# Summing four column groups of a modulation vector with adding transfers in DRAM instead of TensorE transposes

## The chip, the cores and the metric

The kernel runs on one core of a Trainium2 chip. The core has five engines with queues of their own: TensorE (PE in the profile; PEld is its loading of the stationary operand), VectorE (DVE), ScalarE (ACT), GpSimd (POOL) and SyncE (SP, which here only issues transfers). Each engine takes its instructions in order; semaphores hold one back until what it needs is there. The metric is the device time of one execution in microseconds (us).

## The reference

One layer of a hybrid backbone in fp32 over 512 latent tokens of width 1024, with 256 context tokens. What matters here is the modulation: one vector-matrix product gives six vectors of 1024 values, of which the last four (`gt1`, `sh2`, `sc2`, `gt2`) are used late in the layer.

```python
mod = jax.nn.silu(c) @ w_mod[l] + b_mod[l]
sh1, sc1, gt1, sh2, sc2, gt2 = jnp.split(mod[:, None, :], N_MOD, axis=-1)
h_lat = modulate(x, norm1_g[l], sh1, sc1)
...
# the token mixer: Mamba-2 scan and window attention, each projected, gated, then one output projection
out_lat = (g_ssd * (y_ssd @ w_o_ssd) + g_att * (y_att @ w_o_att)) @ w_out
x = x + gt1 * o_lat
x = x + gt2 * conv_ffn(modulate(x, norm2_g[l], sh2, sc2), w_up[l], ...)
return rmsnorm(x, final_g)
```

## The kernel before, in words

**Products.** Every fp32 product is made of three matmuls: each operand is split into a high part (rounded to the PE's fast format) and the rest. `gemm` issues wh x xh (L237), wh x xl (L238) and wl x xh (L240), eight groups of three for a block of 128 rows by 512 tokens: 24 matmuls of 512 columns. Below, such a block is a half of an `os` step (the projection of the scan's output, two halves for each of eight row blocks) or a whole `out` step (the output projection).

**Weights.** They come in pieces of 512 KB. `load_raw` issues one on SP (L177) into a raw buffer, the tile `wraw`, of which there are three; ACT casts it to the high part (`whi`, L183), and DVE subtracts to get the rest (`wlo`, L184). The function of both is `split`. A raw buffer is free, and SP issues the next load, when its last reader has ended.

**The second modulation.** The four late vectors are 4096 values, in eight column groups (cg 0 to 7) of 512. `m_step(i)` is step i of 32; group cg has the steps 4 cg to 4 cg + 3. A step's load (`wm`, 512 KB through the same three raw buffers) carries two blocks of 128 input rows by 512 columns. DVE multiplies each block by a scalar for each partition and adds it to the accumulator `acc`, the tile `tm` (L794 for a group's first block, L796 for the seven others). `tm` has one buffer (L113). After a group's last step `acc` still has to be summed over its 128 partitions: PE transposes it in four pieces into a PSUM bank (L800), DVE sums along the free axis (L802) and adds the bias (L803) into four columns of `mod2`. Groups 0 and 1 give the first gate, 2 and 3 the second norm's shift, 4 and 5 its scale, 6 and 7 the second gate.

**The order of the work.** A list at the end of the program gives the stages: the `os` steps 3 to 7 with the m-steps 10 to 17 woven in (10 with the first, 11 and 12, 13, 14 and 15, 16 and 17), the `out` steps 0 to 4 with the m-steps 18 to 23, `vectors` (which makes the scale vector `a2` of groups 4 and 5), the last `out` steps, the second norm, the `up` steps with the m-steps 24 to 31 beside the first eighteen of them, and the `down` steps. A scheduler then sets each engine's order from dependencies and its own idea of when things are ready; on the chip that order is fixed.

**The merge.** After an `os` step, DVE multiplies by a gate (L1787) and adds the attention branch (L1788), ACT casts the result to `mh` (L1789) and DVE makes the rest `ml` (L1790). Step o gives tile o of `mh` and `ml`; an `out` step reads all eight, tile 7 last. The gates themselves are made by L1780 and L1781 on DVE from rows loaded by SP (L1775).

**The gate as a row.** `row_tiles` takes groups 6 and 7 and needs them along the free axis: PE transposes (L2060), DVE copies (L2061), SP writes 4 KB to DRAM (L2062) and loads rows from there, spread over all partitions (L2067, L2068). It stands beside the third `up` step from the end.

GpSimd's queue has no work between the scan's last use near 743 us and the second norm's near 854 us, and none from there to the down stage.

Of the kernel before, what the change touches and what calls it, by code (L numbers as in the profile page):

```python
# [9 lines left out]
F32 = mybir.dt.float32  # L10
# [3 lines left out]
ALU = mybir.AluOpType  # L14
# [4 lines left out]
P = 128  # L19
# [8 lines left out]
V_BMOD = 0  # L28
# [11 lines left out]
def raw(ap):  # L40
    return ap.bitcast(F32)
# [3 lines left out]
def tile_hybrid_layer(  # L45
# [32 lines left out]
    V, S, G, T = nc.vector, nc.scalar, nc.gpsimd, nc.tensor  # L78
# [5 lines left out]
    dpool = ctx.enter_context(tc.tile_pool(name="dpool", bufs=1, space=DRAM))  # L84
# [25 lines left out]
    def misb():  # L110
        return bank("mis")
# [3 lines left out]
    def tmp(tag):  # L115
        return tpool.tile([P, 512], F32, tag=tag, name=tag, bufs=TMP[tag])
# [27 lines left out]
    for j, t in enumerate((wdn[0], DSUMS[1], DSUMS[2], DSUMS[5], DSUMS[4], wdn[1], wdn[3])):  # L144
        for u in range(DU):
            n = min(2, DK - 2 * u) * HC
# [11 lines left out]
    QUEUED = mybir.DependencyInfo(mybir.DependencyClass.NoSync, mybir.DependencyReason.SCHED_ONLY)  # L158
# [22 lines left out]

    def split(r, n, hi, lo):
        F["cast"] = S.copy(hi[:, :n], r[:, :n])  # L183
        return V.tensor_tensor(lo[:, :n], r[:, :n], raw(hi[:, :n]), ALU.subtract)  # L184

    ELSEWHERE = {}
    SCALED = {("dn", 40), ("dn", 41)}
# [1 line left out]
    def load(key):  # L189
        r, n = load_raw(key)  # L190
        if key[0] == "m":
            return r
        if key in SCALED:
            for z in range(0, n, 512):
                V.tensor_tensor(r[:, z : z + 512], r[:, z : z + 512], rows_["g"][1], ALU.mult)
        if key in ELSEWHERE:
            hi, lo = ELSEWHERE[key]()
            split(r, n, hi, lo)
            return hi, lo
        if key[0] == "dn" and key[1] % 4 > 1:  # L200
            if "dnw" not in F:
                F["dnw"] = hpool.tile([P, 2, 2, 1024], F32R, tag="hll", name="dnw")
            hi, lo = (F["dnw"][:, key[1] % 2, i, :] for i in range(2))
        else:
            hi = wpool.tile([P, 1024], F32R, tag="whi", name="whi", bufs=2)
            lo = wpool.tile([P, 1024], F32R, tag="wlo", name="wlo", bufs=2)
        split(r, n, hi, lo)
        return hi, lo
# [13 lines left out]
    def weave(a, b):  # L222
        r, n, m = [], len(a), len(b)
        for i in range(n):
            r.append(a[i])
            r += b[i * m // n : (i + 1) * m // n]
        return r
# [18 lines left out]
    vec = cpool.tile([P, NV], F32, name="vec")  # L246
# [13 lines left out]
    mod2 = cpool.tile([P, 32], F32, name="mod2")  # L260
# [165 lines left out]
    with tc.tile_pool(name="spool", bufs=1) as sp:  # L426
# [235 lines left out]
        r = {}  # L662
        cq = tmp("te")[:, :LC]
        for j in range(KT):
# [46 lines left out]
            x = ("hi", "lo") if j >= NU else ("hh", "hl")  # L711
# [31 lines left out]
        for n in range(2):  # L743
            for j in range(KT):
                x = ("hi", "lo") if j >= NU else ("hh", "hl")
# [33 lines left out]
        return [("g", i)], fn  # L779

    macc = {}

    def m_step(i):
        cg, kk = i // 4, i % 4

        def fn(r):
            if kk == 0:
                macc[0] = tmp("tm")
            acc = macc[0]
            for u in range(2):  # L790
                k = 2 * kk + u
                sc = csil[:, k, 0:1]
                if k == 0:
                    V.tensor_scalar_mul(acc, r[:, 0:512], sc)  # L794
                else:
                    V.scalar_tensor_tensor(acc, r[:, u * 512 : u * 512 + 512], sc, acc, ALU.mult, ALU.add)  # L796
            if kk == 3:
                ps = misb()
                for c in range(4):
                    T.transpose(ps[:, c * P : (c + 1) * P], acc[:, c * P : (c + 1) * P], ident)  # L800
                z = slice(4 * cg, 4 * cg + 4)
                V.tensor_reduce(mod2[:, z], ps.rearrange("p (c q) -> p c q", c=4), axis=AX.X, op=ALU.add)  # L802
                V.tensor_tensor(mod2[:, z], mod2[:, z], vec[:, V_BMOD + 16 + 4 * cg : V_BMOD + 20 + 4 * cg], ALU.add)  # L803

        return [("m", i)], fn
# [71 lines left out]
    Q, F = {}, {}  # L877
# [957 lines left out]
    a2 = cpool.tile([P, 8], F32, name="a2")  # L1835

    def vectors():
        V.scalar_tensor_tensor(a2, mod2[:, 16:24], 1.0, vec[:, V_N2 : V_N2 + 8], ALU.add, ALU.mult)

    HL = L // 2  # L1840
# [154 lines left out]
    def up_step(t):  # L1995
        def fn(wa, wb):
            pa, pb = accb(), accb()
            if t == 0:

                with tc.manual_schedule(engines={mybir.EngineType.PE}):  # L2000
                    def product(ps, w, k, u):
                        c, z, st, en = slice(k * P, (k + 1) * P), HALF[u], u == 0 and k == 0, k == KT - 1
                        for v, y in ((0, h2h), (1, h2h), (0, h2l)):
                            T.matmul(
                                ps[:, z], w[v][:, c], y[:, k, z],
                                start=st and v == 0 and y is h2h, stop=en and y is h2l, skip_group_check=True,
                            )

                    for k in range(KT):
                        norm2_k(k, 0)  # L2010
                        if k == 2:
                            F["rs2"] = half_root(F["pf"], F["sq2"], 1)
                        if k == 5:
                            F["r2"].append(rms_spread(F["rs2"], 2))
                        product(pa, wa, k, 0)
                        product(pb, wb, k, 0)
                    for k in range(KT):
                        norm2_k(k, 1)
                        product(pa, wa, k, 1)
                        product(pb, wb, k, 1)  # L2020
                a = up_first(pa, pb, t)
            else:
                gemm([(pa, h2h, h2l)], wa)
                a = up_first(pa, pb, t)
                gemm([(pb, h2h, h2l)], wb)
            up_second(a, pb, t)

        return [("up", t), ("up", NFF + t)], fn

    def x1_turn(c):  # L2030

        def fn():
            t = tmp("te")
            V.transpose(t, x1[c // 4][:, c % 4, :])
            for a in range(4):
                o = x1_d[:, c * P + 32 * a : c * P + 32 * a + 32].rearrange("(f i) j -> i f j", i=32)
                nc.sync.dma_start(o, t[32 * a : 32 * a + 32, :].rearrange("i (f j) -> i f j", j=32))

        return [], fn
# [10 lines left out]
    x1_rows = [], x1_load  # L2050
# [3 lines left out]
    rows_ = {}  # L2054

    def row_tiles():
        V.tensor_copy(g2c[:, 0:4], mod2[:, 24:28])
        V.tensor_scalar_mul(g2c[:, 4:8], mod2[:, 28:32], -1.0)
        ps, t = misb(), tmp("te")
        T.transpose(ps[0:8, 0:P], g2c, ident)  # L2060
        V.tensor_copy(t[0:8, 0:P], ps[0:8, 0:P])  # L2061
        nc.sync.dma_start(g2_d.rearrange("(c p) -> c p", p=P), t[0:8, 0:P])  # L2062
        tiles = [hpool.tile([P, HC], F32, tag=t, name="row" + t) for t in ("q2", "ssq", "rbc4")] + [tmp("tm")]
        rows_["g"], rows_["f"] = tiles[:2], tiles[2:]
        for i in range(2):
            z = slice(HC * i, HC * i + HC)
            nc.sync.dma_start(rows_["f"][i], fg_d[z].partition_broadcast(P))  # L2067
            nc.sync.dma_start(rows_["g"][i], g2_d[z].partition_broadcast(P))  # L2068
# [150 lines left out]
    def down_step(j, u):  # L2219
        tail = j == 6 and u == 2  # L2220

        def fn(*w):
# [37 lines left out]
        + weave([os_step(o) for o in range(3, 8)], msteps[10:18])  # L2260
        + weave([out_step(o) for o in range(5)], msteps[18:24])
        + [([], vectors)]
        + [([("out", o) for o in (5, 6, 7)], out_last), ([], close_c1)]
        + weave(
            weave([up_step(t) for t in range(18)], msteps[24:]) + [up_step(t) for t in range(18, NFF)],
            [([], lambda: None)] * 6 + [x1_turn(c) for c in range(8)] + [x1_rows] + [([], lambda: None)] * 4 + [([], row_tiles)] + [([], lambda: None)] * 2,
        )
        + [down_step(j, u) for j in range(7) for u in range(3 if j == 6 else DU)],
        early=("g", 15),
# [86 lines left out]
```

## Time and profile before

| | |
|---|---|
| time, median of 3 runs | 1219.94 us (1219.82 to 1220.01) |
| the profiled execution: time, span | 1219.4 us, 1217.6 us |
| PE busy | 1208.7 us, granted clock 0.998 |
| DVE, ACT, POOL busy | 924.4, 679.6, 204.8 us |
| moved by transfers | 214.71 MB |

The span runs from the first instruction to the last. A line of a group gives the code line, engine, operation, the tile written and the tiles read, and how many; in a timeline the two numbers ahead are start and duration in us, and what stands in brackets is the idle time just before and what ended it. `SPq` and `POOLq` are transfers by the engine that issues them; their time to landing runs from issue to the last byte. Matmul durations overlap, since PE is pipelined: the distance of their starts counts.

### The profile page before, as it was taken

The numbers are of one execution on the slowest core, as the hardware profiler recorded it, in microseconds if no ns is written. First come the engines' busy times: TensorE is split into PE (matmuls) and PEld (weight loads), VectorE is DVE, ScalarE is ACT, GpSimd is POOL, SyncE is SP. The second block draws the span as 40 slices with busy tenths as digits, with TensorE's granted clock in tenths as the row PEclk, the third lists the DMA queues.
The fourth block names the chain that finished last, engine by engine and source line by source line (L and its number), as shares of the span: only waits on it lengthen the run. The fifth ranks groups of instructions, "written<-read, shape, count | busy, mean of one in ns | idle before, by whom it ended". The sixth has DMA issues, their size and how long they took to land.

```text
span 1217.6 us, 17462 instructions
## 1 busy us (share of the span) xinstructions
PE 1208.7 (99%) x6296; PEld 993.7 (82%) x6296; DVE 924.4 (76%) x1499; ACT 679.6 (56%) x1263; POOL 204.8 (17%) x223
## 2 busy tenths in 40 slices
PE   9999999999999999999999999999999999999997
PEld 6798888888878868778777778888988888888886
DVE  5857888888566688797896867677787777768777
ACT  5557787778544367486575664223534334346653
POOL 0000121100003544252451631000200000000021
PEclk9999999999999999999999999999999999999999
DMA  9645889844758535346376558777265534337652
GB/s 371 259 137 184 160 242 261 170 148 129 175 160 247 169 87 181 108 133 194 104 167 202 172 188 277 233 238 242 55 159 135 190 109 135 119 115 234 193 187 88
DMA packets 122920, 214.71 MB, mean 176 GB/s; under 512 B 26312, under 2 KB 68368, under 8 KB 122832
## 3 DMA queue, kind: packets, MB, share of 16 engines
q1 hardware_dynamic: 110256, 187.09, 49.0%
q0 software_dynamic: 12288, 26.22, 9.5%
q8 instruction: 50, 0.82, 0.3%
q14 instruction: 38, 0.31, 0.1%
q10 hardware_dynamic: 288, 0.27, 0.1%
HBM read 187.26 MB, written 43.85 MB: 190 GB/s over the span
## 4 chain that ended last, share of the span: by engine, by line
PE 96%; DVE 1%; issue 1%; ACT 1%; DMA 1%; POOL 0%; SPq 0%; POOLq 0%; DVEq 0%; ACTq 0%
PE acc L237 20%; PE acc L240 20%; PE acc L238 20%; PE score L958 3%; PE po L1007 3%; PE pt L994 2%; PE mis L580 2%; PE mis L1687 2%; PE mis L1559 2%; PE mis L1695 1%; PE mis L2217 1%; PE mis L2216 1%; PE mis L2215 1%; PE acc L2217 1%; PE acc L2216 1%; PE acc L2215 1%
## 5 line engine op out<-in xcount | busy, mean ns | idle before, releaser
L183 ACT CAST whi<-wraw 128x1024 fp32r<-128x1024 f32 (+1 forms) x115 | 120.3, 1047 | 160.0 <-PE acc L238 107.0
L184 DVE TENSOR_TENSOR wlo<-wraw,whi 128x1024 fp32r<-128x1024 f32 (+1 forms) x115 | 143.6, 1249 | 68.1 <-ACT whi L183 65.6
L237 PE MATMUL acc<-hlh,whi 128*128 128x512 f32 x472 | 194.0, 411 | 0.0
L238 PE MATMUL acc<-hll,whi 128*128 128x512 f32 x472 | 185.0, 392 | 0.0
L240 PE MATMUL acc<-hlh,wlo 128*128 128x512 f32 x472 | 184.9, 392 | 0.0
L237 PE MATMUL acc<-mh,whi 128*128 128x512 f32 x368 | 143.6, 390 | 0.0
L238 PE MATMUL acc<-ml,whi 128*128 128x512 f32 x368 | 143.2, 389 | 0.0
L240 PE MATMUL acc<-mh,wlo 128*128 128x512 f32 x368 | 143.2, 389 | 0.0
L240 PEld LDWEIGHTS acc<-hlh,wlo 128*128 128x128 f32 x472 | 88.6, 188 | 19.6
L237 PEld LDWEIGHTS acc<-hlh,whi 128*128 128x128 f32 x472 | 88.8, 188 | 18.0 <-issue 2.8
L238 PEld LDWEIGHTS acc<-hll,whi 128*128 128x128 f32 x472 | 88.9, 188 | 17.3 <-issue 2.4
L240 PEld LDWEIGHTS acc<-mh,wlo 128*128 128x128 f32 x368 | 69.1, 188 | 14.5
L237 PEld LDWEIGHTS acc<-mh,whi 128*128 128x128 f32 x368 | 69.1, 188 | 14.4
L238 PEld LDWEIGHTS acc<-ml,whi 128*128 128x128 f32 x368 | 69.1, 188 | 14.2
L967 DVE CUSTOM_DVE_ANT_0 p<-score,winm,nsink 128x512 f32<-128x512 f32 (+1 forms) x64 | 51.8, 810 | 15.4 <-PE score L958 13.9
L1392 DVE SCALAR_TENSOR_TENSOR ta<-acc,half,ta 128x511 f32<-128x511 f32 (+1 forms) x66 | 43.8, 664 | 22.6 <-ACT ta L1391 22.4
L1391 ACT ACTIVATE ta<-acc,half 128x512 f32<-128x512 f32 (+1 forms) x66 | 46.7, 708 | 25.2 <-PE acc L240 23.9
L974 ACT ACTIVATE p<-p,mneg 128x512 f32<-128x512 f32 (+1 forms) x64 | 49.7, 777 | 15.4 <-DVE mneg L967 14.8
L164 POOL DMA_DIRECT2D dsum<-wdn x24 | 25.4, 1143 | 193.0 <-DVE wlo L1091 171.7
L1002 DVE TENSOR_TENSOR ptl<-pt,pth 128x512 fp32r<-128x512 f32 x72 | 47.5, 685 | 8.5 <-ACT pth L998 7.7
L796 DVE SCALAR_TENSOR_TENSOR tm<-wraw,csil,tm 128x512 f32<-128x512 f32 x56 | 43.6, 778 | 13.0 <-DMA wraw<-wm 12.3
L237 PE MATMUL acc<-hch,whi 128*128 128x256 f32 x176 | 53.2, 302 | 0.0
(444 smaller groups left out, 2994.0 us busy)
## 6 DMA issues: line engine op xcount, KB each, us to landing
wraw<-wup SPq DMA_DIRECT2D x44, 512.0 KB, 3.6
dsum<-wdn POOLq DMA_DIRECT2D x24, 704.0 KB, 8.9
wraw<-wm SPq DMA_DIRECT2D x32, 512.0 KB, 4.0
fb<-cs_d SPq DMA_DIRECT2D x32, 512.0 KB, 6.6
wraw<-wx SPq DMA_DIRECT2D x24, 512.0 KB, 3.7
wm<-wm SPq DMA_DIRECT2D x16, 512.0 KB, 8.2
wraw<-wz SPq DMA_DIRECT2D x16, 512.0 KB, 4.2
wraw<-wos SPq DMA_DIRECT2D x16, 512.0 KB, 4.7
```

The costliest lines, as they stand in the source:

```text
L183: F["cast"] = S.copy(hi[:, :n], r[:, :n])
L184: return V.tensor_tensor(lo[:, :n], r[:, :n], raw(hi[:, :n]), ALU.subtract)
L237: T.matmul(ps, wh, xh[:, k0 + k, :], start=a, stop=False)
L238: T.matmul(ps, wh, xl[:, k0 + k, :], start=False, stop=False)
L240: T.matmul(ps, wl, xh[:, k0 + k, :], start=False, stop=b)
L796: V.scalar_tensor_tensor(acc, r[:, u * 512 : u * 512 + 512], sc, acc, ALU.mult, ALU.add)
L958: T.matmul(ps[:, o : o + len(z) * P], Q[h][:, b * P : (b + 1) * P], k[:, j, z[0] * P : (z[-1] + 1) * P], start=v == 0 and o % 512 in (0, P ...
L967: V.tensor_tensor_reduce(p[:, :w], d["ps"][i][:, o0 : o0 + w], m, op0=ALU.add, op1=ALU.min, scale=1.0, scalar=nsink[:, h : h + 1], accum_o ...
L974: S.activation(p, p, AF.Exp, bias=d["mneg"][:, i : i + 1], scale=-1.0, accum_out=d["den"][:, i : i + 1])
L1002: V.tensor_tensor(d["ptl"][x], d["pt"][x], raw(d["pth"][x]), ALU.subtract)
L1391: S.activation(o[:, :n], ps[:, :n], AF.Identity, scale=hcol(base_w, stride + i), bias=hcol(base_b, i))
L1392: x = V.scalar_tensor_tensor(o[:, 1:n], ps[:, 0 : n - 1], hcol(base_w, i), o[:, 1:n], ALU.mult, ALU.add)
```

## The change

Groups 2, 3, 6 and 7 are no longer summed by PE. When such a group's accumulator is complete, `fold` issues nine transfers on GpSimd's queue: one copies `acc` (128 rows of 512 values, 256 KB) to a DRAM tile, seven add the lower half of the rows onto the upper half (64, 32, 16, 8, 4, 2 and 1 rows, `max_dma_last_dim=512` setting the size of their pieces), and one brings the remaining row into four columns of `mod2`. Each waits for the landing of the one before. The bias addition is a function of its own, `folded`, placed later in the program: group 2's in step 20, group 6's in step 31, group 3's in `vectors`, group 7's in `row_tiles`; in the scheduler's order it stands behind the latest split. `row_tiles` itself stands two places later, beside the last `up` step.

```diff
     def split(r, n, hi, lo):
         F["cast"] = S.copy(hi[:, :n], r[:, :n])
-        return V.tensor_tensor(lo[:, :n], r[:, :n], raw(hi[:, :n]), ALU.subtract)
+        F["sub"] = V.tensor_tensor(lo[:, :n], r[:, :n], raw(hi[:, :n]), ALU.subtract)
+        return F["sub"]
...
+    FOLDS = {cg: dpool.tile([P, 512], F32, name="fold%d" % cg) for cg in (2, 3, 6, 7)}
+
+    def fold(cg, acc):
+
+        d, n = FOLDS[cg], P // 2
+        G.dma_start(d, acc)
+        while n:
+            G.dma_start(d[0:n, :], d[n : 2 * n, :], accum_op=ALU.add, max_dma_last_dim=512)
+            n //= 2
+        G.dma_start(mod2[:, 4 * cg : 4 * cg + 4], d[0, :].rearrange("(c p) -> p c", p=P))
+
+    def folded(cg):
+        z = slice(4 * cg, 4 * cg + 4)
+        x = V.tensor_tensor(mod2[:, z], mod2[:, z], vec[:, V_BMOD + 16 + 4 * cg : V_BMOD + 20 + 4 * cg], ALU.add)
+        tc.add_manual_dep(x.ins, F["sub"].ins.name, QUEUED, reason="behind a split")
...
-            if kk == 3:
+            if i in (20, 31):
+                folded({20: 2, 31: 6}[i])
+            if kk == 3 and cg in FOLDS:
+                fold(cg, acc)
+            elif kk == 3:
                 ps = misb()
...
     def vectors():
+        folded(3)
...
     def row_tiles():
+        folded(7)
...
-            [([], lambda: None)] * 6 + [x1_turn(c) for c in range(8)] + [x1_rows] + [([], lambda: None)] * 4 + [([], row_tiles)] + [([], lambda: None)] * 2,
+            [([], lambda: None)] * 6 + [x1_turn(c) for c in range(8)] + [x1_rows] + [([], lambda: None)] * 6 + [([], row_tiles)],
```

The new code moves the lines behind it by some twenty: L794 and L796 become L810 and L812, L1780, L1781, L1787, L1788 and L1790 become L1800, L1801, L1807, L1808 and L1810; L184 stays. On GpSimd's queue the first fold (of group 2) now stands where nothing stood, between the first and the second norm's work; its rows, with the tile `fold` in DRAM and `mod` for `mod2`:

```order
L788 DMA fold_764<-tm 128x512
L790 DMA fold_764<-fold_764 256x128
L790 DMA fold_764<-fold_764 128x128
L790 DMA fold_764<-fold_764 64x128
L790 DMA fold_764<-fold_764 32x128
L790 DMA fold_764<-fold_764 16x128
L790 DMA fold_764<-fold_764 16x64
L790 DMA fold_764<-fold_764 16x32
L792 DMA mod_94<-fold_764 128x4x1
```

Group 3's nine follow directly.

The change also moves DVE's rows. The first place is the middle of `os` steps 6 and 7. Before, from a split of step 6's second weight on, with the four multiplies of the m-steps 14 and 15 (L796, reading `tm` and `wraw`) between splits (L184) and merge operations:

```order
L184 TENSOR_TENSOR wlo<-wraw,whi 128x1024
L796 SCALAR_TENSOR_TENSOR tm<-wraw,csil,tm 128x512
L1787 TENSOR_TENSOR tb<-acc,ld_7598 128x512
L184 TENSOR_TENSOR wlo<-wraw,whi 128x1024
L1788 TENSOR_TENSOR tb<-tb,ld_7600 128x512
L796 SCALAR_TENSOR_TENSOR tm<-wraw,csil,tm 128x512
L1790 TENSOR_TENSOR ml<-tb,mh 128x512
L796 SCALAR_TENSOR_TENSOR tm<-wraw,csil,tm 128x512
L1781 SCALAR_TENSOR_TENSOR ld_7598<-ld_7598,r_s 128x512
L796 SCALAR_TENSOR_TENSOR tm<-wraw,csil,tm 128x512
L184 TENSOR_TENSOR wlo<-wraw,whi 128x1024
```

Now, with the first row step 14's first multiply and the second row the same split as the first row above:

```order
L812 SCALAR_TENSOR_TENSOR tm<-wraw,csil,tm 128x512
L184 TENSOR_TENSOR wlo<-wraw,whi 128x1024
L812 SCALAR_TENSOR_TENSOR tm<-wraw,csil,tm 128x512
L1807 TENSOR_TENSOR tb<-acc,ld_7602 128x512
L812 SCALAR_TENSOR_TENSOR tm<-wraw,csil,tm 128x512
L1808 TENSOR_TENSOR tb<-tb,ld_7604 128x512
L184 TENSOR_TENSOR wlo<-wraw,whi 128x1024
L1810 TENSOR_TENSOR ml<-tb,mh 128x512
L812 SCALAR_TENSOR_TENSOR tm<-wraw,csil,tm 128x512
L1801 SCALAR_TENSOR_TENSOR ld_7602<-ld_7602,r_s 128x512
L1800 SCALAR_TENSOR_TENSOR ld_7604<-ld_7603,ld_7604 128x512
L184 TENSOR_TENSOR wlo<-wraw,whi 128x1024
```

Step 14 has moved from behind that split to ahead of it, and step 15's first multiply from behind the next split to ahead of it.

The second place is the passage from the last `os` step to `out` step 0, on DVE again. Before, from the split of `out` step 0's weight (first row) to the end of the last merge (L1787, L1788, L1790), with the m-steps 18 (second row) and 19 (last row):

```order
L184 TENSOR_TENSOR wlo<-wraw,whi 128x1024
L796 SCALAR_TENSOR_TENSOR tm<-wraw,csil,tm 128x512 x2
L1787 TENSOR_TENSOR tb<-acc,ld_7598 128x512
L1788 TENSOR_TENSOR tb<-tb,ld_7600 128x512
L184 TENSOR_TENSOR wlo<-wraw,whi 128x1024
L1790 TENSOR_TENSOR ml<-tb,mh 128x512
L796 SCALAR_TENSOR_TENSOR tm<-wraw,csil,tm 128x512 x2
```

Now:

```order
L812 SCALAR_TENSOR_TENSOR tm<-wraw,csil,tm 128x512
L184 TENSOR_TENSOR wlo<-wraw,whi 128x1024
L812 SCALAR_TENSOR_TENSOR tm<-wraw,csil,tm 128x512
L1807 TENSOR_TENSOR tb<-acc,ld_7602 128x512
L812 SCALAR_TENSOR_TENSOR tm<-wraw,csil,tm 128x512
L1808 TENSOR_TENSOR tb<-tb,ld_7604 128x512
L184 TENSOR_TENSOR wlo<-wraw,whi 128x1024
L1810 TENSOR_TENSOR ml<-tb,mh 128x512
L812 SCALAR_TENSOR_TENSOR tm<-wraw,csil,tm 128x512
```

Step 18's first multiply has moved ahead of that split, and step 19's between the two halves of the last merge.

## The prediction

> **What bounds the kernel now.** I read the page's head and its chain first: who is busy, and what the end hangs on.
>
> ```profile
> span 1217.6 us, 17462 instructions
> PE 1208.7 (99%) x6296; PEld 993.7 (82%) x6296; DVE 924.4 (76%) x1499; ACT 679.6 (56%) x1263; POOL 204.8 (17%) x223
> PE 96%; DVE 1%; issue 1%; ACT 1%; DMA 1%; POOL 0%; SPq 0%; POOLq 0%; DVEq 0%; ACTq 0%
> ```
>
> TensorE (PE) carries 96% of the chain and never rests. So only two things move the time: PE instructions that go away, and new moments in which PE waits. Then I read the stages in which the change works, by windows, and the transfers of 755 to 845 us, where the second modulation's loads run between the projections' weights.
>
> ```profile
> core 0: us, PE busy (x) PEld busy (x) DVE busy (x) ACT busy (x) POOL busy (x), PEclk, DMA share, GB/s
> 757.00:779.00 22.00, 22.00 (x99) 18.22 (x98) 14.95 (x21) 5.46 (x6) 0.00 (x0) 1.00 0.70 226
> 779.00:801.00 22.00, 22.00 (x101) 18.19 (x100) 14.60 (x22) 5.44 (x6) 0.00 (x0) 1.00 0.75 236
> 801.00:823.00 22.00, 22.00 (x101) 18.19 (x100) 16.99 (x23) 5.99 (x7) 0.00 (x0) 1.00 0.80 251
> ...
> 1060.00:1105.00 45.00, 45.00 (x202) 37.15 (x201) 32.67 (x49) 18.07 (x25) 0.00 (x0) 1.00 0.38 118
> ```
>
> PE is busy for all of each window, POOL (GpSimd) is idle, DVE has a quarter of its time free, and the transfers are dense (0.70 to 0.80) in the first three, thin (0.38) in the up stage.
>
> ```profile
> wraw<-wm SPq DMA_DIRECT2D x13, 512.0 KB, 4.5
> wraw<-wos SPq DMA_DIRECT2D x8, 512.0 KB, 5.0
> ...
> DMA to landing us min/median/max: 3.5/4.7/5.6
> ...
> DVE tm L796 <- DMA wraw<-wm: 2.5, 1, 2.5
> ```
>
> A load of 512 KB takes 4.5 to 5 us here, 3.5 at the best and 5.6 at the worst. Once, DVE stood 2.5 us before an m-step's load, in order, with a weight's split queued behind it. That wait cost PE nothing then; how near it was to costing is the question.
>
> **What is taken away.** One group of transposes, by the timeline of PE:
>
> ```profile
> 779.59 0.39 PE L240 MATMUL acc<-yh,wlo 128*128 128x512 f32 x1
> 779.82 0.60 PE L800 MATMUL mis<-ident,tm 128*128 128x128 f32 x4
> 780.17 0.48 PE L237 MATMUL acc<-yh,whi 128*128 128x512 f32 x1
> 780.49 0.40 PE L238 MATMUL acc<-yl,whi 128*128 128x512 f32 x1
> 780.72 0.40 PE L240 MATMUL acc<-yh,wlo 128*128 128x512 f32 x1
> ...
> 791.64 0.39 PE L240 MATMUL acc<-yh,wlo 128*128 128x512 f32 x1
> ```
>
> Matmuls otherwise start 0.227 apart (779.59, 779.82), so L240 would have come at 780.28 instead of 780.72: 0.44 us a group. Four groups go (column groups 2, 3, 6, 7): 4 x 0.44 = 1.8 us, all of it on PE's path. Four of DVE's sums behind them go too, and their bias additions stay:
>
> ```profile
> 780.62 0.68 DVE L802 TENSOR_REDUCE mod<-mis 128x4 f32<-128x512 f32 x1
> ...
> 781.82 0.15 DVE L803 TENSOR_TENSOR mod<-mod,vec 128x4 f32<-128x4 f32 x1
> ```
>
> 4 x 0.68 us on DVE are worth nothing by themselves, since DVE isn't the bound. The gain of 1.8 us is 0.15%, less than the 0.2% (2.4 us) that a measurement of this kernel can tell from no change.
>
> **What is moved: DVE's order.** This decides. The accumulator tile `tm` has one buffer. Before, PE had to transpose it before the next column group could start; now it is free when the copy to DRAM has landed, and the scheduler places the m-steps of group 3 one projection half earlier: in the rows of the order, step 14's first multiply stood behind the split of the half that PE needs at 791.64, and now stands ahead of it; step 15's stands ahead of the next split, step 18's ahead of out_step 0's, step 19's ahead of the last merge's second half. Each of these waits for a load, and DVE goes in order. And each load is issued only when a raw buffer is free: step 14's when the split before has ended, step 15's when the split behind step 14 has. So load, multiply, split and load form a loop that has to fit in one half of a projection (24 matmuls x 0.2275 = 5.46 us).
>
> ```profile
> 769.59 0.75 DVE L796 SCALAR_TENSOR_TENSOR tm<-wraw,csil,tm 128x512 f32<-128x512 f32 x1
> ...
> 770.97 0.69 DVE L1788 TENSOR_TENSOR tb<-tb,ld 128x512 f32<-128x512 f32 x1
> 771.58 1.22 DVE L184 TENSOR_TENSOR wlo<-wraw,whi 128x1024 fp32r<-128x1024 f32 x1
> ...
> 775.96 0.69 DVE L1781 SCALAR_TENSOR_TENSOR ld<-ld,r_s 128x512 f32<-128x512 f32 x1 [2.56 <-DMA ld<-ts_d]
> ```
>
> With these durations (successive operations overlap by about 0.08), and L for a load:
> - Step 14: L + 0.75 + 1.22 - 0.08 = L + 1.9. Step 15, with L1788 between: L + 2.5. They fit for L under 3.6 and under 3.0.
> - The start: step 12's second multiply comes behind L1781, at 776.57, and ends at 777.3; step 13's load goes out then. Step 13's two multiplies, L1787, L1788 and the split follow its landing: 777.3 + L + 3.75.
>
> I take L = 4.4, just below the median of the m loads: while DVE waits, it frees no buffer, and fewer loads share the engines. Then:
> 1. The split behind step 13 ends at 785.5. PE needs it at 785.76 (5.44 before 791.20, which is 791.64 less the 0.44 of the group that is gone). No stall.
> 2. Step 14: 785.5 + 6.3 = 791.85 against 791.20: 0.65.
> 3. Step 15: 791.85 + 6.9 = 798.75 against 791.85 + 5.46 = 797.3: 1.45.
> 4. Steps 16 and 17: two halves with one late load between, 0 to 1; I take 0.3.
> 5. Step 18 ahead of out_step 0's split: L + 1.9 = 6.3 against 5.46: 0 to 0.85; 0.6.
> 6. Step 19 ahead of the merge. Its rows before:
>
> ```profile
> 813.89 0.39 PE L240 MATMUL acc<-mh,wlo 128*128 128x512 f32 x1
> ...
> 818.20 0.39 PE L237 MATMUL acc<-mh,whi 128*128 128x512 f32 x1
> ...
> 815.45 0.69 DVE L1788 TENSOR_TENSOR tb<-tb,ld 128x512 f32<-128x512 f32 x1
> ...
> 817.20 0.68 DVE L1790 TENSOR_TENSOR ml<-tb,mh 128x512 fp32r<-128x512 f32 x1
> ...
> 816.18 0.62 ACT L1789 CAST mh<-tb 128x512 fp32r<-128x512 f32 x1 [0.98 <-DVE tb L1788]
> ```
>
> PE takes the last of mh's eight tiles 4.31 after out_step 0's split is first used (818.20 - 813.89). Step 19's load is issued when that split ends; mh then needs L + 0.75 + 0.69 + 0.62 = 6.45: late by 2.1; ml comes 0.8 after that beyond PE's next step. Together 2.9 if the split was just in time, less if it had slack; I take 2.5.
>
> Sum: 0.65 + 1.45 + 0.3 + 0.6 + 2.5 = 5.5 of stalls, less 1.8: +3.7 us. The profiled execution took 1219.4 (span 1217.6 and 1.8 around it), 0.5 below the median 1219.94; on the median that gives 1223.6.
>
> Bounds. At L = 3.5 the splits of steps 14 and 15 come at 790.0 and 796.0, in time, and only the merge's wait may be left: 0 to 1. At L = 5.6 the five terms are about 1 + 2 (step 14), 2.6, 1.5, 2 and 4: 13. Against the median: 1218.2 to 1231.
>
> **What is added.** Each fold is nine transfers in a row on GpSimd's queue. No row shows an adding transfer of this size; the nearest are POOL's own:
>
> ```profile
> dsum<-wdn POOLq DMA_DIRECT2D x24, 704.0 KB, 8.9
> ...
> DMA to landing us min/median/max: 3.1/3.2/4.6
> ...
> DMA to landing us min/median/max: 1.8/3.5/7.8
> ...
> L794 DVE TENSOR_SCALAR tm<-wraw,csil x3: 478/479/483, 781.9 to 827.7; 128x512 f32<-128x512 f32 x3
> ...
> L184 DVE TENSOR_TENSOR wlast<-wraw,wlast x3: 1224/1225/1227, 838.9 to 842.8; 128x1024 fp32r<-128x1024 f32 x3
> ```
>
> The first line is of 704 KB transfers that partly add; the second is of the loads of `xs` from DRAM (256 KB), the third of the stores of `xs_d` (64 and 32 KB, eight issued at a time, hence the 7.8). A link of a fold is issued alone: between 1.8 and 4.6 us, 3.2 taken, since its largest has 256 KB too. Nine make a fold of 16 to 41, likely 29. Fold 2 starts at 770.4 (L796 of 769.59 ends 770.34): its copy lands at 773.6, ahead of L1781, so step 12 is not held; it ends near 799, its reader stands behind step 20's first multiply, the last of the three L794 (827.7). Fold 3 starts near 800 (798.75 and the 1.4 of step 15's second multiply and L1790) and ends near 829; DVE takes it among the three wlast splits (838.9 to 842.8). Folds 6 and 7 lie in the up stage, where the order of the m-steps hardly moves. The four bias additions replace four of the same size (0.15). All are hidden by PE's matmuls as long as a link stays under 4.3.
>
> The gate row's transpose moves from 1083 to the end of the up stage:
>
> ```profile
> 1104.85 0.39 PE L240 MATMUL acc<-mh,wlo 128*128 128x512 f32 x1
> ...
> 1105.05 1.05 ACT L183 CAST whi<-wraw 128x1024 fp32r<-128x1024 f32 x1 [0.62 <-PE acc L238]
> ...
> 1106.14 1.22 DVE L184 TENSOR_TENSOR wlo<-wraw,whi 128x1024 fp32r<-128x1024 f32 x1 [0.98 <-ACT whi L183]
> ```
>
> The transpose comes behind that L240, the up stage's last; the copy L2061 then waits on DVE until about 1104.85 + 0.6 (the row of L800) = 1105.5, ahead of this split, before which DVE stands idle 0.98 us until 1106.1 for ACT anyhow: nothing. The row loads on SP now fall among the down weights; their readers come much later. If that cover is gone, under 1 us.
>
> **Rivals.**
> A. The waits vanish: with DVE held, loads run nearly alone and land in 3.5 to 4. For it: the row's minimum 3.5. Against it: m and wos loads have medians 4.5 and 5.0, and the fold adds traffic. Then only the transposes count: 1219.94 - 1.8 + 0 to 1.5 = 1218.2 to 1219.7, within 0.2%. It decides from L = 3.6 downwards for step 14, and up to L = 4.1 the net stays within 0.2%. Chance 0.32.
> B. The chain of a fold is so long that fold 3's copy, queued on POOL behind fold 2's ninth issue, keeps `tm` from step 16: at 4.6 a link the ninth issue comes at 770.4 + 8 x 4.6 = 807 instead of 800, some 6 us on top: 1230. It begins at 3.7. The POOL issues themselves varied (dsum: 0.515 to 2.132 us):
>
> ```profile
> L164 POOL DMA_DIRECT2D dsum<-wdn x24: 515/1246/2132, 91.7 to 325.4; - x24
> ```
>
> The Trainium skill ("SBUF — State Buffer", section "SBUF: two separate sides") says that a VectorE operation in a two-port mode locks GpSimd out of the port by which it writes descriptors, so that its transfers starve. By that rule each link would lengthen towards the longest issue here, and the time would be this rival's 1230; no trace of before shows the two together in this stage. Chance 0.05.
> C. The folds' own traffic slows the weights: 0.5 MB each, written and read again, in a stage that moves 226 to 251 GB/s. At 0.3 us more per load the five terms grow by about 0.3 x 6: 1225.5; that is inside my range. The Trainium skill ("DMA: Bandwidth & Descriptors", section "Issuing engines are not separate DMA queues") says that transfers of all issuing engines run interleaved on the same 16 engines; by it this load is shared, not free, and the time would be nearer 1225.5 than 1223.6. Chance 0.08.
> D. A group of transposes costs its whole 0.60 and both seams: 4 x 0.7 = 2.8, with no stall: 1217.1, faster. Against it: the starts give 0.44. Chance 0.04.
>
> **How the numbers follow.** My forecast (L between 4.1 and 5) 0.51: 1223.6, its own range 1221.5 to 1227. With B and C, slower by over 0.2%: 0.51 x 0.97 + 0.05 + 0.08 = 0.63. Within 0.2%: A and a rest, 0.33. Faster: 0.04. The range takes in A's low end, and from L = 5.6 and B all but the last tenth: 1218.0 to 1229.
>
> **What would show it.** PE in 755 to 830 with idle time before L240 and, at the merge, before L237 and L238 of mh and ml, released by DVE L184 and L1790; DVE with several waits for wm loads instead of one of 2.5; the largest at step 19. The PE rows of the transposes halved. If DVE waits for wm loads and PE still has no gap, the loop is looser than I put it. If `tm` is released late, step 12 or 16 shows a wait for POOL's copy, and B holds.

## The result, and the profile after

The changed kernel takes 1229.26 us (median of 6 runs, 1228.25 to 1230.13), beside 1219.88 for the kernel before on the same chips: ratio 1.0077, 95% interval 1.0064 to 1.009. It is slower by 9.4 us. The profiled execution has a span of 1227.4 us, 9.8 more than before.

The head of the page and its chain:

```profile
span 1227.4 us, 17468 instructions
PE 1210.5 (99%) x6280; PEld 992.9 (81%) x6280; DVE 919.9 (75%) x1495; ACT 679.7 (55%) x1263; POOL 234.2 (19%) x259
PE 89%; DMA 5%; DVE 3%; issue 2%; ACT 1%; POOL 1%; SPq 0%; POOLq 0%; DVEq 0%; ACTq 0%
```

The sixteen transposes are gone (6296 to 6280), but PE's busy time grew by 1.8 us, and DMA, which carried 1% of the chain, carries 5%. The windows say where:

```profile
core 0: us, PE busy (x) PEld busy (x) DVE busy (x) ACT busy (x) POOL busy (x), PEclk, DMA share, GB/s
757.00:779.00 22.00, 22.00 (x99) 18.21 (x98) 15.64 (x23) 5.46 (x6) 1.63 (x2) 1.00 0.74 239
779.00:801.00 22.00, 19.33 (x83) 15.03 (x82) 12.85 (x17) 5.10 (x6) 3.91 (x5) 1.00 0.74 218
801.00:823.00 22.00, 18.16 (x73) 14.35 (x72) 11.07 (x16) 3.73 (x5) 4.69 (x6) 0.92 0.70 211
823.00:845.00 22.00, 20.36 (x90) 16.27 (x89) 14.65 (x22) 5.75 (x8) 3.89 (x5) 1.00 0.67 214
```

Before, PE was busy for 22.00 of each 22. Now 8.15 us are lost in three windows, and in one of them its clock was lower (0.92). The waits of PE between 755 and 850 us, and the two largest of DVE between 764 and 830:

```profile
PE acc L241 <- DVE wlo L184: 6.5, 4, 3.8
PE acc L238 <- ACT mh L1809: 1.1, 1, 1.1
PE acc L239 <- DVE ml L1810: 0.6, 1, 0.6
...
DVE tm L812 <- DMA wraw<-wm: 12.1, 5, 3.2
DVE tm L810 <- DMA fold<-tm: 10.3, 2, 7.6
```

(The three matmuls of a product are L238, L239 and L241 now.) PE waits for splits and for the last merge. DVE, in front of these, waits for two things: five times for an m-step's load, and twice for a copy to DRAM to give `tm` free. DVE's timeline shows both kinds:

```profile
777.04 0.49 DVE L810 TENSOR_SCALAR tm<-wraw,csil 128x512 f32<-128x512 f32 x1 [2.64 <-DMA fold<-tm]
...
783.71 1.54 DVE L812 SCALAR_TENSOR_TENSOR tm<-wraw,csil,tm 128x512 f32<-128x512 f32 x2 [3.18 <-DMA wraw<-wm]
...
802.93 1.22 DVE L184 TENSOR_TENSOR wlo<-wraw,whi 128x1024 fp32r<-128x1024 f32 x1
811.76 0.49 DVE L810 TENSOR_SCALAR tm<-wraw,csil 128x512 f32<-128x512 f32 x1 [7.62 <-DMA fold<-tm]
...
814.34 1.22 DVE L184 TENSOR_TENSOR wlo<-wraw,whi 128x1024 fp32r<-128x1024 f32 x1
```

At 811.76 step 16 starts, 7.62 us after DVE was free; the split behind it ends at 815.56, and PE had wanted it at 811.6. The copy that it waited for is the second of these (POOL's timeline):

```profile
771.63 0.64 POOL L788 DMA_DIRECT2D fold<-tm  x1 [28.52 <-DVE tm L812]
777.31 0.99 POOL L790 DMA_DIRECT2D fold<-fold  x1 [5.04 <-DMA fold<-tm]
...
808.28 0.83 POOL L792 DMA_DIRECT2D mod<-fold  x1 [4.29 <-DMA fold<-fold]
809.10 0.58 POOL L788 DMA_DIRECT2D fold<-tm  x1
```

Group 3's accumulator was complete at about 801.8, but its copy stood behind group 2's eight landings and was issued at 809.10. From 771.63 to 808.28 are 36.65 us for eight links, 4.6 each (from one issue to the next).

### The profile page after: what moved, and what is told of

It reads as the page before. It is cut to its first block, busy times and chain, and to the rows that moved or that the text cites. A ratio compares the mean times of both kernels' runs of the same rounds, so it can differ in the third digit from the quotient of the medians.

```text
span 1227.4 us, 17468 instructions
## 1 busy us (share of the span) xinstructions
PE 1210.5 (99%) x6280; PEld 992.9 (81%) x6280; DVE 919.9 (75%) x1495; ACT 679.7 (55%) x1263; POOL 234.2 (19%) x259
## 4 chain that ended last, share of the span: by engine, by line
PE 89%; DMA 5%; DVE 3%; issue 2%; ACT 1%; POOL 1%; SPq 0%; POOLq 0%; DVEq 0%; ACTq 0%
PE acc L238 18%; PE acc L239 18%; PE acc L241 18%; PE score L978 3%; PE po L1027 3%; PE pt L1014 2%; PE mis L581 2%; PE mis L1707 2%; DMA fold<-fold 2%; PE mis L1579 2%; PE mis L1715 1%; PE mis L2238 1%; PE mis L2239 1%; PE mis L2237 1%; PE acc L2239 1%
## 5 line engine op out<-in xcount | busy, mean ns | idle before, releaser
L238 PE MATMUL acc<-hlh,whi 128*128 128x512 f32 x472 | 193.9, 411 | 0.0
L184 DVE TENSOR_TENSOR wlo<-wraw,whi 128x1024 fp32r<-128x1024 f32 (+1 forms) x115 | 143.6, 1249 | 62.9 <-ACT whi L183 59.8
L241 PE MATMUL acc<-hlh,wlo 128*128 128x512 f32 x472 | 184.9, 392 | 0.0
L239 PE MATMUL acc<-hll,whi 128*128 128x512 f32 x472 | 184.9, 392 | 0.0
L238 PE MATMUL acc<-mh,whi 128*128 128x512 f32 x368 | 143.4, 390 | 1.1 <-ACT mh L1809 1.1
L239 PE MATMUL acc<-ml,whi 128*128 128x512 f32 x368 | 143.3, 389 | 0.6 <-DVE ml L1810 0.6
L241 PE MATMUL acc<-mh,wlo 128*128 128x512 f32 x368 | 143.3, 389 | 0.0
L241 PEld LDWEIGHTS acc<-hlh,wlo 128*128 128x128 f32 x472 | 88.6, 188 | 19.6
L238 PEld LDWEIGHTS acc<-hlh,whi 128*128 128x128 f32 x472 | 88.8, 188 | 17.9 <-issue 2.8
L239 PEld LDWEIGHTS acc<-hll,whi 128*128 128x128 f32 x472 | 88.9, 188 | 17.3 <-issue 2.4
L238 PEld LDWEIGHTS acc<-mh,whi 128*128 128x128 f32 x368 | 69.1, 188 | 15.7 <-ACT mh L1809 1.5
L239 PEld LDWEIGHTS acc<-ml,whi 128*128 128x128 f32 x368 | 69.1, 188 | 15.1 <-DVE ml L1810 0.9
L241 PEld LDWEIGHTS acc<-mh,wlo 128*128 128x128 f32 x368 | 69.1, 188 | 14.8 <-DVE wlo L184 0.4
L812 DVE SCALAR_TENSOR_TENSOR tm<-wraw,csil,tm 128x512 f32<-128x512 f32 x56 | 43.5, 777 | 21.4 <-DMA wraw<-wm 20.9
L241 PE MATMUL acc<-yh,wlo 128*128 128x512 f32 x120 | 47.9, 399 | 6.5 <-DVE wlo L184 6.5
```

What stands on the lines that cost most here:

```text
L184: F["sub"] = V.tensor_tensor(lo[:, :n], r[:, :n], raw(hi[:, :n]), ALU.subtract)
L238: T.matmul(ps, wh, xh[:, k0 + k, :], start=a, stop=False)
L239: T.matmul(ps, wh, xl[:, k0 + k, :], start=False, stop=False)
L241: T.matmul(ps, wl, xh[:, k0 + k, :], start=False, stop=b)
```

## The experiments

Two causes stood against each other, and a third beside them. The order: m-steps placed earlier on DVE, whose loads it awaits ahead of the splits. The hold: `tm` kept by a copy that is queued behind another chain. The traffic: adding transfers that lengthen the weight loads. The kernel before took 1219.8 to 1220.0 us beside all of these runs.

**1. Only the groups of the up stage (e1_up_only).**

```diff
-    FOLDS = {... for cg in (2, 3, 6, 7)}
+    FOLDS = {... for cg in (6, 7)}
...
-            if i in (20, 31):
-                folded({20: 2, 31: 6}[i])
+            if i == 31:
+                folded(6)
...
     def vectors():
-        folded(3)
```

> Only groups 6 and 7 (the up stage) are folded; groups 2 and 3 keep TensorE's transposes, and DVE's order between the projections is that of the kernel before. If the loss comes from the place of groups 2 and 3 (the order of the m-steps, and the copy that holds tm), it is gone, and two groups of transposes are saved: 1219.9 - 0.9 = 1219.0 us. If adding transfers cost wherever they run, by their traffic, some of the loss stays: above 1220.5 us.

Measured: 1218.35 us, ratio 0.9989 (0.998 to 0.9997). All of the loss is gone, and some gain is left; 0.9 lies inside the interval. The loss belongs to groups 2 and 3. In the up stage, where the order hardly moves and the transfers are thinner, a fold shows no cost.

**2. All folds, with the order of the kernel before and a tile of its own for group 3 (e3_order).** `F["h", o]` is the second merge operation (L1788 before) of `os` step o.

```diff
-                macc[0] = tmp("tm")
+                macc[0] = hpool.tile([P, 512], F32, tag="ssq", name="tm_b") if cg == 3 else tmp("tm")
...
-                    V.tensor_scalar_mul(acc, r[:, 0:512], sc)
+                    x = V.tensor_scalar_mul(acc, r[:, 0:512], sc)
+                    if cg in (3, 4):
+                        tc.add_manual_dep(x.ins, F["h", 2 * cg - 2].ins.name, QUEUED, reason="behind a merge")
...
-                    V.scalar_tensor_tensor(acc, r[:, u * 512 : u * 512 + 512], sc, acc, ALU.mult, ALU.add)
+                    x = V.scalar_tensor_tensor(acc, r[:, u * 512 : u * 512 + 512], sc, acc, ALU.mult, ALU.add)
+                    if (i, u) == (19, 0):
+                        tc.add_manual_dep(x.ins, F["h", 7].ins.name, QUEUED, reason="behind a merge")
...
     def vectors():
-        folded(3)
...
     def close_c1():
+        folded(3)
```

> The changed kernel with all four folds, but group 3's accumulator in a tile of its own, so that no copy holds tm for step 16, and the first multiplies of groups 3 and 4 and of step 19 held behind the merges of the os steps 4, 6 and 7, where they stood before; group 3's bias is added after the last out steps. All transfers of the change remain. If order and hold make the loss: 1219.9 - 1.8 = 1218.1 us, with no gap of PE between 755 and 845 us. If the traffic of the folds makes it: 1222 us or more.

Measured: 1217.59 us, ratio 0.998 (0.9971 to 0.9989). It is faster than both kernels. Its trace has DVE's order of the kernel before, but for neighbours that changed places near 794 and 801 us. Its windows:

```profile
779.00:801.00 22.00, 22.00 (x99) 18.22 (x98) 14.30 (x20) 5.47 (x6) 3.91 (x5) 1.00 0.82 250
801.00:823.00 22.00, 22.00 (x99) 18.15 (x98) 16.17 (x21) 6.00 (x7) 3.91 (x5) 1.00 0.89 285
```

PE is busy throughout, with the same 36 transfers on POOL's queue and a higher DMA share (0.89) than in either kernel. The traffic doesn't make the loss.

**3. The early order without any fold (e4_before_acc3):** the kernel before with group 3's accumulator in the tile of its own (the first edit of 2, on the kernel before).

> The kernel before, all eight sums by TensorE and nothing on GpSimd's queue, with group 3's accumulator in a tile of its own. The scheduler then places the m-steps of group 3 as early as in the changed kernel. If DVE's waits for the m-steps' loads, ahead of the splits, make a part of the loss by themselves: PE stalls of 4 to 6 us, 1223 to 1226 us. If the loss needs the folds (their traffic or their chain): 1219.9 us.

Measured: 1223.49 us, ratio 1.0032 (1.0021 to 1.0042). Its waits of PE and DVE in the same stretches:

```profile
PE acc L237 <- ACT mh L1789: 1.5, 1, 1.5
...
DVE tm_b L796 <- DMA wraw<-wm: 5.3, 3, 2.5
DVE tm L796 <- DMA wraw<-wm: 4.6, 3, 2.9
DVE tm L794 <- DMA wraw<-wm: 2.6, 1, 2.6
...
DVE tm_b L794 <- DMA wraw<-wm: 0.9, 1, 0.9
```

Nothing runs on GpSimd's queue, all transposes are still there, and a second buffer for one accumulator costs 3.7 us: DVE waits eight times for m-step loads, and the last merge comes late. The order makes a loss by itself. (It isn't row by row that of the changed kernel: step 12's first multiply stands earlier, and the rows of the steps 17 to 19 stand otherwise among the splits.)

**4. The chain cut to two links (e6_no_adds).**

```diff
         G.dma_start(d, acc)
-        while n:
-            G.dma_start(d[0:n, :], d[n : 2 * n, :], accum_op=ALU.add, max_dma_last_dim=512)
-            n //= 2
```

> The changed kernel without the seven adding transfers of each fold: the copy to DRAM is followed at once by the transfer into mod2, so the sum over partitions is left out. DVE's order is that of the changed kernel. The chain of a fold has two links instead of nine, and group 3's copy isn't held behind group 2's chain. If the hold makes 5.5 us (4.0 of wait and 1.5 of slow matmuls behind it): 1229.3 - 5.5 = 1223.8 us, with DVE still waiting for m-step loads. If the early order costs nothing by itself: 1218.1 us.

Measured: 1224.11 us, ratio 1.0033 (1.0021 to 1.0045). 5.2 us of the 9.4 go with the long chain, the rest stays. DVE still waits 4.0 us at step 16 here, for the copy's own landing, so this is not yet the order alone:

```profile
DVE tm L809 <- DMA wraw<-wm: 11.3, 6, 3.8
DVE tm L807 <- DMA fold<-tm: 6.9, 2, 4.0
```

**5. The hold alone (e7_hold):** 2 without its first edit, so that `tm` has one buffer for all groups; group 3's bias inside the second norm.

```diff
                     for k in range(KT):
+                        if k == 4:
+                            folded(3)
                         norm2_k(k, 0)
```

> DVE's order of the kernel before with all four folds, and tm with its one buffer; group 3's bias is added within the second norm. Only the hold is left: step 16 can't start before group 3's copy has landed, and the copy stands behind group 2's chain until about 811 us, where the kernel before starts step 16 at 806.6. The split of out step 0 behind steps 16 and 17 then ends at about 815.4 against a need at 813.0, and the last merge is late by another 2 to 3: 1217.6 + 5 = 1222.6 us. If the early order alone makes the loss: 1217.6 us.

Measured: 1221.71 us, ratio 1.0014 (1.0005 to 1.0023). DVE's wait, and PE behind it:

```profile
DVE tm L810 <- DMA fold<-tm: 6.1, 1, 6.1
...
813.04 0.39 PE L239 MATMUL acc<-ml,whi 128*128 128x512 f32 x1
815.47 0.79 PE L241 MATMUL acc<-mh,wlo 128*128 128x512 f32 x1 [2.04 <-DVE wlo L184]
816.06 0.63 PE L238 MATMUL acc<-mh,whi 128*128 128x512 f32 x1
```

Against 2 the hold costs 4.1 us, and 3.6 against 9, which differs from this kernel in nothing but the tile of group 3's accumulator. The trace has the split late by 2.2 (815.47 - 813.04 - 0.23), against 2.4 expected. The late merge that I had added to it didn't come; in its place PE ran at half speed behind the wait (starts 0.43 us apart, 816.06 and the rows after it), for 1.7 us more.

**6. The hold taken away, the early order kept (e5_early_own):** the changed kernel with the first edit of 2 and the late bias of 5.

> The changed kernel with group 3's accumulator in a tile of its own and the late bias: the hold is gone, the early order and all transfers stay. Beside e4_before_acc3 (1223.5 us, the same early order without any fold) it shows the price of the folds' traffic: 1223.5 - 1.8 = 1221.7 us if it costs nothing, 1223 us or more if it lengthens the loads on which DVE waits.

Measured: 1224.42 us, ratio 1.0034 (1.002 to 1.0047), 4.8 us under the changed kernel and 2.7 over the 1221.7 expected (experiment 3 less the gain of the transposes). That spoke for the traffic, so it was taken away alone. The order isn't quite kept: with no hold at step 12 either, its first multiply stands ahead of a split and a merge behind which it stood in the changed kernel, and step 13's rows stand a little otherwise; from step 14 on the rows are the same.

**7. Experiment 6 without the adding transfers (e10_own_no_adds),** by the edit of 4.

> e5_early_own without the seven adding transfers of each fold (the sum over partitions is left out); DVE's order is row by row that of e5_early_own. The difference to its 1224.4 us is the price of the adding transfers beside the weight loads. If they cost what the two kernels of early order differ by: 1224.4 - 2.7 = 1221.7 us. If they cost nothing, and the rest of the order makes that difference: 1224.4 us.

Measured: 1224.02 us, ratio 1.0032 (1.002 to 1.0045). DVE's order is the same row by row, and 0.4 us is far inside the intervals: no price of the adding transfers shows, though one of up to some 2 us could hide in them. The waits of PE here:

```profile
PE acc L241 <- DVE wlo L184: 2.4, 3, 1.3
PE acc L238 <- ACT mh L1806: 1.2, 1, 1.2
PE acc L2021 <- ACT mh L1954: 1.1, 1, 1.1
...
PE acc L239 <- DVE ml L1807: 0.6, 1, 0.6
```

The third line lies near 871 us, in the second norm, behind the stretch of the m-steps 12 to 19. The traces of 5, 6, 7, 9 and 10, in which group 3's bias is added inside the second norm, all show this wait, and those of the changed kernel and of 2 and 3 don't. So up to 1.1 of the 2.7 can belong to the late bias. The rest is left to the order, which in experiment 3 is another from step 17 on; that difference wasn't tried apart.

This is the nearest there is to the kernel of the prediction's sum, early order and no hold, and it stands 0.4 us above the time forecast, with the 1.1 of the late bias in it. From the distances of PE's starts, the splits and the merge cost 0.1 (step 14), 0.6 (step 15), 0.7 (steps 16 and 17), 1.5 (step 18) and 2.2 (the merge): 5.1, where the sum has 0.65, 1.45, 0.3, 0.6 and 2.5. That the sums lie so near is in part luck.

**8. The gate rows alone (e8_rows_late),** two places later in the kernel before (the last line of the change).

> The kernel before with the gate rows alone two places later. The copy waits on DVE inside an idle stretch, and the row loads have late readers: 1219.8 us, within 0.3. If their place among the down weights' loads costs: above 1220.5 us.

Measured: 1219.49 us, ratio 0.9997 (0.9988 to 1.0006). That part shows no cost.

**9. Experiment 2 with the late bias of 5 (e9_late_bias).**

> e3_order with group 3's bias added within the second norm, just ahead of its first reader, so that DVE no longer waits 3.5 us for the end of group 3's chain at 851 us, nor PE 0.7 us behind it: 1217.6 - 0.7 = 1216.9 us. If that wait of PE was covered anyhow: 1217.6 us.

Measured: 1218.13 us, ratio 0.9985 (0.9976 to 0.9994), not to be told from 2. PE's wait of 0.5 us near 853 is gone, but another of 1.1 us came near 866, within the second norm. No gain.

**10. The hold taken away by another queue (e11_sp_copy):** experiment 5 with the copies on SyncE.

```diff
-        G.dma_start(d, acc)
+        nc.sync.dma_start(d, acc)
```

> e7_hold with the four copies to DRAM on SyncE's queue instead of GpSimd's, so that group 3's copy doesn't stand behind group 2's chain. DVE's order of the kernel before, one buffer for tm. If that place in the queue alone makes the hold: 1221.7 - 4.1 = 1217.6 us, as e3_order. If SyncE, waiting for the accumulator ahead of weight loads, delays these: 1219 us or more.

Measured: 1218.55 us, ratio 0.9987 (0.9978 to 0.9996). With the copy out of the chain's queue the hold is gone, with one buffer. Between this and the 1217.59 of experiment 2, or the 1218.13 of experiment 9, the intervals overlap.

## Why the prediction was right and wrong

Right: the direction, the place and the mechanism of the order, though its single terms were off in both directions. Slower was given 0.63. Measured is 1229.26 against 1223.6, and 0.26 us above the range. Wrong: the length of a fold's link, and with it the hold, which was left out of the sum.

- **The transposes.** The gain of 1.8 us is there: 2.2 in experiment 2, interval 1.3 to 3.5.
- **DVE's order.** The sum of the stalls was 5.5 us. In the changed kernel, from the distances of PE's starts: 1.5 at the split behind step 13 (0 forecast), 0.9 at step 14 (0.65), 0.7 at step 15 (1.45), 0.1 at step 18 (0.6), 2.1 at the merge (2.5): 5.3. That these add up to the forecast is in part luck. The loops behave as written, but one L for all loads doesn't hold: the loads of the steps 13, 14, 15, 18 and 19 took 4.8, 4.6, 3.7, 5.1 and 3.5 us. For step 15, 3.7 + 2.5 - 5.46 is 0.74. Step 18's 5.1 would give 1.5, as in experiment 7; here PE was late by the hold already and needed the split later. The 1.5 at step 13 came from the first copy and a load together: the copy was issued at 771.63, 1.2 later than put down, and landed 5.4 us after its issue and not 3.2, so that step 12 started at 777.04; step 13's load then took 4.8. In experiment 4 a copy just as slow, issued earlier, with a load of 3.5 behind it cost no stall there. Without hold and adds nearly the same order takes 1224.0 (experiment 7).
- **The step that failed is "3.2 taken" for a link of a fold.** A link of the first fold measured 4.6 with the 0.3 us from a landing to the next issue, which I had left out; it is the upper end that I had written, and past the 3.7 from which rival B begins. (The prediction also has a limit of 4.3; that one holds only for the readers of `mod2`, while the limit for `tm` is the lower one.) So B came on top of the forecast, where I had made it an alternative at 0.05. Its price, "some 6 us", came out near, in part by luck: the trace has 4.0 us of wait at 811.38 and 1.5 of slow matmuls behind it, which the prediction didn't have; by the experiments 3.6 to 4.8 (5 and 6). The other way to B, long issues on GpSimd, didn't come: the folds' issues took 0.57 to 0.99 us. With the stalls of 5.3 and the 1.8 of the transposes these make 5.3 + 4.0 + 1.5 - 1.8 = 9.0 of the 9.4 measured. The number 3.2 was taken from a row of loads near 400 us, while in the stage itself the loads on SP took a third longer in the median than at their best (4.7 against 3.5), and I had that row before me.
- **Rival A** fell as a whole: the m loads landed in 4.5 (median) as before, and the waits didn't vanish. But two of the five loads on which the sum rests, those of the steps 15 and 19, landed in the 3.5 to 4 that A had. **C** isn't seen: the m loads are no slower than before, and without the adds the time is the same within the intervals. **D** fell as a forecast, since the time rose; its 0.7 for a group lies inside the intervals of experiments 1 and 2.
- **The gate rows** at nothing: right (experiment 8). The bias additions at nothing: right, DVE waits for none of them in the changed kernel.

## What to carry to other kernels

A buffer that comes free earlier is not free of cost under a scheduler: work that was held back by it moves forward in an in-order queue, and if that work waits for transfers, it carries its waits ahead of what the bounding engine needs. When a chain of dependent transfers goes onto a queue, the first transfer of the next chain stands behind all of it, and whatever buffer it was to empty stays taken for that long. Price a link by transfers of the stage in which it will run, with the time from a landing to the next issue, and let two unlikely-looking costs add up before the range is closed.

## What the runs showed of the hardware

Behind a long wait PE works at half speed for a while. The changed kernel, PE's timeline behind step 16's wait:

```profile
811.38 0.39 PE L239 MATMUL acc<-yl,whi 128*128 128x512 f32 x1
815.61 0.79 PE L241 MATMUL acc<-yh,wlo 128*128 128x512 f32 x1 [3.84 <-DVE wlo L184]
816.20 0.63 PE L238 MATMUL acc<-yh,whi 128*128 128x512 f32 x1
816.63 0.63 PE L239 MATMUL acc<-yl,whi 128*128 128x512 f32 x1
...
818.34 0.55 PE L241 MATMUL acc<-yh,wlo 128*128 128x512 f32 x1
818.72 0.39 PE L238 MATMUL acc<-yh,whi 128*128 128x512 f32 x1
```

The starts are 0.43 us apart instead of 0.23 until 818.7, some 3 us, and the granted clock of the window from 801 to 823 us is 0.92. It cost 1.5 us. The same came behind single waits of 2.1, 2.2 and 3.2 us (experiments 4, 5 and 6), and not behind waits of 1.6 us and less (experiments 3 and 7). So a stall of 2 us or more of PE cost some 1.5 to 1.7 us beyond itself here. The Trainium skill ("TensorE: Matmul & The Clock Gate", section "Part 1: The HAM clock gate (the "warmup" mystery)") says that the clock halves after an idle window of about 3.4 us and returns after about as much sustained work; the return agrees with the 3 us seen, while the drop came here after waits of 2.1 and 2.2 us, less than that window.

A small adding transfer on GpSimd's queue costs nearly what a large one costs: from 128 KB down to 2 KB the medians (of two transfers for each size) were 3.0 to 5.9 us from issue to landing between 765 and 845 us, with no trend by size, and the shortest of the whole execution took 2.0. From issue to issue, the mean link of a fold that adds in this stage, over the changed kernel and experiments 2, 5, 6 and 9, was 3.5 to 4.9 us, at a DMA share of 0.65 to 0.89; in the up stage, at a share near 0.4, it was 3.2 to 3.9.
